# List writes issued per group, the first expert's weight splits behind the routing, and an earlier read of the sums in a fused mixer and expert kernel

## The chip, the cores and the metric

The kernel runs on one core of one Trainium2 chip. The metric is device time in microseconds (us) of one execution; a kernel is run several times, and the median counts. TensorE is called PE, VectorE DVE, ScalarE ACT, GpSimd POOL and SyncE SP, as in the profile.

## The reference

One transformer-like block over 2048 tokens of width 1024. A norm and a projection feed two mixers (a chunked linear-attention mixer and a delta-rule mixer), whose outputs are gated, projected and added to x. Then comes a hierarchical mixture of experts: of 4 groups the best one is taken, in it the best 2 of 8 experts, by softmax weights. Cut to what matters here:

```
x   = x + gt1 * (mixed @ w_out)
h2  = rmsnorm(x, norm2_g) * (1 + sc2) + sh2
lg  = h2 @ wg_r + bg_r;   grp = argmax(lg);   p_grp = softmax(lg)[grp]
pe  = softmax((h2 @ we_r + be_r)[grp]);       top2 of pe -> experts, weights
for each expert e and each token t sent to it:
    hid = silu(h2[t] @ w_gate[e]) * (h2[t] @ w_up[e])     # 1024 -> 512
    out[t] += weight * (hid @ w_down[e])                  # 512 -> 1024
x   = x + gt2 * out
return rmsnorm(x, final_g)
```

All is float32. There are 32 experts, and each has three weight matrices of 2 MB.

## The kernel before

A product in float32 is made of three matmuls on rounded halves: a matrix W is split into `whi` (ACT's cast) and `wlo` (DVE's subtraction W - whi). `Moe.halves` does this for a piece of 128 x 1024; an expert has 12 pieces (`RING` = 12 pairs of halves are kept), four rows of gate and up each and four of down.

The kernel has three phases that matter here. **Mid** (class `Mid`) goes over 16 tiles of 128 tokens: `tile(i)` multiplies by w_out, `after(j)` writes the row block to `X2` (in the profile: X), transposes it, makes the norm and the routing logits `lg`, and writes h2 to `H2` (H). When a group of tiles of `GROUPS` = (0,4), (4,4), (8,4), (12,2), (14,1), (15,1) (first tile, count) has its logits, `route` makes a long chain of small DVE instructions: softmax, best group, best two experts, the mask `M` of chosen experts, with two PE products the place of each token in its expert's list, and from it the row numbers `di`. For each tile two indirect DMAs on POOL then write the token number and weight into the list of its expert in memory (`LIST`), 32 writes in all. The order of instructions in Mid is set by a scheduler.

**Moe.run** follows, whose order is as written. SP loads the first three experts' lists; POOL gathers the first expert's rows of h2 by its list (`gather`) into `gx`; PE transposes them (`x_turn`), ACT and DVE split them (`x_split` into xh, xl); then `block(e)` runs for the 32 experts. `past` inside the block runs a further block on tokens beyond 128 (names `ih`, `il`, "inner"), if the expert has so many. Each expert's result y is added to `X2` by an indirect DMA on POOL (`add`).

Weights come through a ring: `load_next` issues a load of one piece (512 KB) into a `raw` tile, `split` turns it into halves, `pump(n)` does n splits and one load behind each. `todo` lists the 32 x 12 pieces and then the 16 row blocks of `X2`, which are loaded only once `summed` is set. `Moe.first`, called in Mid at tile 15, loads `RAW` = 7 pieces and does all 12 splits of the first expert; `LATE` = 8 more raw tiles exist in Moe.run, whose loads are issued on ACT's queue behind the first `x_split`.

**The tail**: as `X2` may be read once the adds are in, its 16 row blocks are normed in groups of four (`split` of e = NE: ACT squares in `roots`, POOL power, DVE multiplication in `norm`, SP write of the output) beside the last expert's block. Expert 29's add had to be in before the reads; expert 30's y is kept and added behind the reads (`late`); expert 31's y is never added to memory. The tokens of experts 30 and 31 are instead gathered from `X2` by their lists (`sums`), 31's y is added in place, they are normed and written over the output rows by an indirect DMA (`place`), in `last_rows`.

Of the kernel before, what the change touches and what calls it, by code (L numbers as in the profile page):

```python
# [6 lines left out]
FP = mybir.dt.float32  # L7
# [4 lines left out]
OP = mybir.AluOpType  # L12
AX = mybir.AxisListType
# [851 lines left out]
class Mid:  # L865
# [103 lines left out]
    def run(s, ctx):  # L969
        s.moe.lasting()  # L970
        s.k.md = s.t = ctx.enter_context(s.k.tc.tile_pool(name="md", bufs=1, side="right"))
        s.rows()
        s.consts()
        xs, n, due = s.xs, len(s.xs), []
        for i in range(n, 17):
            if i < 15:
                s.tokens(i + 1)
            if i < 16:
                xs[i] = s.tile(i)
            if i == 15:  # L980
                s.moe.first()
            for j in [j for j in sorted(xs) if j < i]:
                i0, c = [(i0, c) for i0, c in GROUPS if i0 <= j < i0 + c][0]
                if j == i0:
                    lg = s.t.tile([128, 4, 36], FP, name="lg", bufs=4)
                s.after(j, xs.pop(j), lg[:, j - i0])
                if j == i0 + c - 1:
                    due.append((i0, c, lg))
                if due and (j >= sum(due[0][:2]) - 1 + (0 if due[0][0] > 8 else 3)):
                    route(s.k, *due.pop(0), s.moe.ps)  # L990
        for d in due:
            route(s.k, *d, s.moe.ps)

# [15 lines left out]
def route(k, i0, c, lg, ps):  # L1009

    nc, md = k.nc, k.md
    T = lambda n, *sh: md.tile([128, 4, *sh], FP, name=n, bufs=4)[:, :c]
# [54 lines left out]
    for j, e in enumerate(E):  # L1067
# [12 lines left out]
        for i in range(c):  # L1080
            one = nc.gpsimd.indirect_dma_start(
                out=k.LIST, out_offset=bass.IndirectOffsetOnAxis(ap=di[:, i:i + 1], axis=0),
                in_=row[:, i], in_offset=None)

            for other in k.scat:
                k.tc.declare_no_dep(one.ins, other.ins, reason="other rows")
            k.scat.append(one)


class Moe:  # L1090
    RING, RAW, LATE = 12, 7, 8

# [29 lines left out]
    def first(s):  # L1122

        for _ in range(min(s.RAW, len(s.todo))):
            s.load_next()
        s.pump(s.RING)

# [21 lines left out]
    def counts(s):  # L1149
        pt = s.ps.tile([128, 512], FP, name="tr", bufs=4)  # L1150
        s.nc.tensor.matmul(pt[:, 0:32], s.k.ones, s.k.Msum, start=True, stop=True)
        s.nc.vector.tensor_copy(s.cnt, pt[0:1, 0:32])

        s.nc.vector.tensor_reduce(s.most, pt[0:1, 30:32], AX.X, OP.max)

# [45 lines left out]
    def last_rows(s):  # L1201


        k, nc, NE = s.k, s.nc, s.k.NE
        xs = [s.raws.pop((NE, j)) for j in range(12, 16)]
        rs = s.roots(xs)
        ls = [s.lists[:, e, 0] for e in (NE - 2, NE - 1)]
        gs = [s.sums(l) for l in ls]
        y = s.own()
        s.norm(xs, rs)  # L1210
        for j, x in enumerate(xs):
            nc.sync.dma_start(s.O[0, (12 + j) * 128:(13 + j) * 128, :], x)
        nc.vector.tensor_tensor(gs[1], gs[1], y, OP.add)
        s.norm(gs)
        for l, x in zip(ls, gs):
            s.place(l, x)

# [48 lines left out]
    def block(s, e, lst, xh, xl, inner=False, mid=None, turn=None):  # L1266
# [14 lines left out]
        for k2 in range(4):  # L1281
            for j, P in enumerate((G, U)):
                prod(P, j, 2 * k2)
                prod(P, j, 2 * k2 + 1)
                if 0 < k2 < 3:
                    pump(1)
            if end and k2 in (1, 2):
                s.pump(4)
            if k2 == 0 and mid:
                mid()  # L1290
                if e == k.NE - 1:
                    s.junk = s.gx[2]
# [22 lines left out]
        if end:  # L1315
            s.pump(4)
            s.late.pop()()
        Y = s.banks(("Y0", "Y1"), inner)
        for kk in range(4):
# [4 lines left out]
            if kk < 3:  # L1324
                pump(1)
        late = e == k.NE - 2 and not inner
        y = s.gx[(e + 1) % 2] if late else s.t.tile([128, 1024], FP, name="y", bufs=2)

# [32 lines left out]
    def run(s, O):  # L1361
# [29 lines left out]
        if NE > 1:  # L1391
            xs.append(first(1))
        hl = s.x_tiles()
        for q in range(2):
            s.x_split(s.x_turn(xs[0], q), *hl, q)
        for _ in range(s.LATE):
            s.load_next(nc.scalar)
        second(0)
        for e in range(NE):
# [43 lines left out]
            hl = nxt  # L1443
            if e >= NE - 3:
                s.summed = True
                while s.loaded < min(s.done + s.RAW + s.LATE, len(s.todo)):
                    s.load_next()
        s.last_rows()

        with tc.If(most > 128):  # L1450
            for e in (NE - 2, NE - 1):
                n = nc.values_load(s.cnt[0:1, e:e + 1], min_val=0, max_val=2048)
# [118 lines left out]
```

## Time and profile before

| | |
|---|---|
| median of three runs | 2954.5 us (2951.3 to 2956.52) |
| the profiled execution | 2948.01 us, of which the span from first to last instruction 2946.2 us |
| mean granted clock of PE in it | 0.967 |
| PE busy | 2724.7 us, 92% of the span |
| DVE / ACT / POOL busy | 2013.0 / 1274.6 / 798.2 us |
| bytes moved | 734.25 MB, mean 249 GB/s |

The profiled execution is one run, somewhat below the median of the three others. Busy shares are means over phases with different limits; what a change is worth is read at its own place. In the profile an instruction's row gives its start and its duration, the tile it writes and reads, and in brackets how long its engine had been idle before it and what released it.

### The profile page before, as it was taken

How to read it: one execution, taken by the hardware profiler on the slowest of the kernel's cores; microseconds unless marked ns; L12 is line 12 of the kernel's file. 1: busy time of each engine (PE TensorE's matmuls, PEld its weight loads, DVE VectorE, ACT ScalarE, POOL GpSimd, SP SyncE). 2: the span in 40 equal slices, each digit the busy share in tenths (PEclk: the TensorE clock that was granted, in tenths of full speed). 3: DMA queues.
4: the chain of work that ended last, by engine and by line, in shares of the span. 5: the costliest groups of instructions: out<-in, count | busy, mean ns of one | idle time of the engine just before them, and what ended most of it. 6: DMA issues, size and time to landing. Idle time of an engine off the chain costs nothing. (4 is left out here: it accounts for less than half of the span.)

```text
span 2946.2 us, 45527 instructions
## 1 busy us (share of the span) xinstructions
PE 2724.7 (92%) x15434; PEld 2245.7 (76%) x15434; DVE 2013.0 (68%) x4136; ACT 1274.6 (43%) x2183; POOL 798.2 (27%) x983
## 2 busy tenths in 40 slices
PE   6989999999999999999999999899958999999993
PEld 5767787878888888888888878688857777777772
DVE  6374775683676656587647886436565699988984
ACT  4333443342333523333333544322225577767763
POOL 2011322322332312342233343322341112111111
PEclk9989999999999999999999989999979999999996
DMA  8999775577565776566665767976448799999996
GB/s 268 305 335 286 236 236 166 181 240 230 158 209 183 235 240 206 179 219 206 203 198 172 233 207 255 345 271 216 144 151 257 272 364 367 362 331 370 366 320 249
DMA packets 460586, 734.25 MB, mean 249 GB/s; under 512 B 115553, under 2 KB 277345, under 8 KB 460242
## 3 DMA queue, kind: packets, MB, share of 16 engines
q1 hardware_dynamic: 448114, 696.68, 70.7%
q0 software_dynamic: 10976, 29.21, 4.3%
q10 hardware_dynamic: 1152, 4.19, 0.4%
q8 instruction: 164, 2.69, 0.4%
q14 instruction: 180, 1.47, 0.2%
HBM read 561.81 MB, written 175.00 MB: 250 GB/s over the span
## 5 line engine op out<-in xcount | busy, mean ns | idle before, releaser
L778 PE MATMUL mm<-hThi,w 128*128 128x512 f32 x1472 | 592.8, 403 | 16.0 <-ACT hThi L667 10.0
L780 PE MATMUL mm<-hThi,w 128*128 128x512 f32 x1472 | 589.5, 401 | 0.2 <-DVE w L761 0.2
L779 PE MATMUL mm<-hTlo,w 128*128 128x512 f32 x1472 | 588.2, 400 | 0.0
L1240 DVE TENSOR_TENSOR wlo<-raw,whi 128x1024 fp32r<-128x1024 f32 x404 | 483.0, 1252 | 45.3 <-ACT whi L1239 29.2
L1239 ACT CAST whi<-raw 128x1024 fp32r<-128x1024 f32 x408 | 405.6, 1057 | 204.0 <-PE U L931 47.9
L778 PEld LDWEIGHTS mm<-hThi,w 128*128 128x128 f32 x1472 | 280.4, 190 | 85.2 <-ACT hThi L667 10.1
L780 PEld LDWEIGHTS mm<-hThi,w 128*128 128x128 f32 x1472 | 280.4, 191 | 65.2 <-DVE w L761 6.6
L779 PEld LDWEIGHTS mm<-hTlo,w 128*128 128x128 f32 x1472 | 280.2, 190 | 57.4 <-DVE hTlo L668 0.7
L1340 POOL DMA_INDIRECT X<-y,lists x32 | 70.8, 2213 | 484.7 <-DVE y L1332 447.5
L243 DVE TENSOR_TENSOR pr<-Pl,Nl 128x2 f32<-128x2 f32 (+30 forms) x496 | 184.9, 373 | 11.7
L451 POOL TENSOR_TENSOR Xq<-h,kf 128x256 f32<-128x256 f32 x96 | 80.1, 834 | 379.7 <-ACT h L448 128.8
L761 DVE TENSOR_TENSOR w<-wraw,w 128x512 fp32r<-128x512 f32 x108 | 80.5, 746 | 106.6 <-ACT w L760 106.6
L760 ACT CAST w<-wraw 128x512 fp32r<-128x512 f32 x108 | 66.6, 619 | 163.4 <-DMA wraw<-in_w_in_dram 103.7
L244 DVE TENSOR_REDUCE Pl<-pr 128x1 f32<-128x2 f32 (+30 forms) x496 | 124.3, 251 | 12.6
L296 PE MATMUL xy<-UV,Gc 128*64 128x64 f32 (+1 forms) x1536 | 115.3, 225 | 3.0 <-ACT UV L305 3.0
L1270 PE MATMUL G<-whi,xh 128*128 128x512 f32 x256 | 104.1, 407 | 11.3 <-PEq L1413 8.6
L296 PEld LDWEIGHTS xy<-UV,Gc 128*64 128x64 f32 (+1 forms) x1536 | 97.2, 128 | 20.2 <-issue 5.9
L856 PE MATMUL mm<-hThi,w 128*128 128x512 f32 x256 | 104.1, 410 | 7.6 <-DMA w<-Ww_proj_b 2.6
L857 PE MATMUL mm<-hTlo,w 128*128 128x512 f32 x256 | 103.9, 406 | 2.6 <-DVE hTlo L668 2.6
L858 PE MATMUL mm<-hThi,w 128*128 128x512 f32 x256 | 102.3, 400 | 0.0
L1270 PE MATMUL G<-whi,xl 128*128 128x512 f32 x256 | 100.7, 393 | 0.0
L1270 PE MATMUL G<-wlo,xh 128*128 128x512 f32 x256 | 100.6, 393 | 0.0
(495 smaller groups left out, 5798.9 us busy)
## 6 DMA issues: line engine op xcount, KB each, us to landing
raw<-in_exp_w_gate_dram SPq DMA_DIRECT2D x126, 512.0 KB
raw<-in_exp_w_up_dram SPq DMA_DIRECT2D x126, 512.0 KB
raw<-in_exp_w_down_dram SPq DMA_DIRECT2D x124, 512.0 KB
w<-Whg SPq DMA_DIRECT2D x96, 512.0 KB
w<-Wgt SPq DMA_DIRECT2D x96, 512.0 KB
w<-Wrw SPq DMA_DIRECT2D x84, 512.0 KB
wraw<-in_w_in_dram SPq DMA_DIRECT2D x92, 256.0 KB
Whg<-w SPq DMA_DIRECT2D x32, 512.0 KB
```

The costliest lines, as they stand in the source:

```text
L243: nc.vector.tensor_tensor(pv, Pl[:, :ni, :ns], Nl[:, :ns, t_][:, None, :].to_broadcast([128, ni, ns]), OP.mult)
L244: nc.vector.tensor_reduce(Pl[:, :ni, t_], pv, AX.X, OP.add)
L296: mm = lambda *a_, **kw: nc.tensor.matmul(*a_, skip_group_check=True, **kw)
L778: nc.tensor.matmul(pt, whi, hi[kk // 2][:, kk % 2], start=(kk == 0), stop=False)
L779: nc.tensor.matmul(pt, whi, lo[kk // 2][:, kk % 2], start=False, stop=False)
L780: nc.tensor.matmul(pt, wlo, hi[kk // 2][:, kk % 2], start=False, stop=(kk == 7))
L856: nc.tensor.matmul(pt, w[:, 0, kk], hi[o // 2][:, o % 2], start=(kk == 0), stop=False)
L857: nc.tensor.matmul(pt, w[:, 0, kk], lo[o // 2][:, o % 2], start=False, stop=False)
L858: nc.tensor.matmul(pt, w[:, 1, kk], hi[o // 2][:, o % 2], start=False, stop=(kk == 3))
L1239: s.nc.scalar.copy(hi, raw)
L1240: eng.tensor_tensor(lo, raw, hi.bitcast(FP), OP.subtract)
L1270: mm = lambda *a, **kw: nc.tensor.matmul(*a, skip_group_check=True, **kw)
```

## The change

It has three parts. First, `route` returns its LIST writes as functions instead of issuing them; `Mid.run` issues them group by group, groups of four are routed two tiles earlier, a group of fewer is routed at once even if another came due at the same tile, and writes that come due at tile 14 are held to tile 15. Second, `Moe.first` only loads; the 12 splits of the first expert stand in Moe.run, six ahead of the first `x_split` and six behind it, and the `LATE` loads (7 now) are issued on SP right behind the list loads. Third, `X2` is read behind expert 28's add; experts 29 and 30 are both kept and added behind the reads (POOL, in the last block), three lists are gathered, two of them are normed in the last block, and the last one behind it.

```diff
@@ class Mid: run
+                while due and (j >= sum(due[0][:2]) - 1 + (0 if due[0][0] > 8 else 1)):
+                    rows += route(s.k, *due.pop(0), s.moe.ps)
+                if j < 14 or j == 15:
+                    for r in rows:
+                        r()
+                    rows = []
-                if due and (j >= sum(due[0][:2]) - 1 + (0 if due[0][0] > 8 else 3)):
-                    route(s.k, *due.pop(0), s.moe.ps)
-        for d in due:
-            route(s.k, *d, s.moe.ps)
@@ route
         for i in range(c):
-            one = nc.gpsimd.indirect_dma_start(
-                out=k.LIST, out_offset=bass.IndirectOffsetOnAxis(ap=di[:, i:i + 1], axis=0),
-                in_=row[:, i], in_offset=None)
...
+            def write(di=di[:, i:i + 1], row=row[:, i]):
+                one = nc.gpsimd.indirect_dma_start(
+                    out=k.LIST, out_offset=bass.IndirectOffsetOnAxis(ap=di, axis=0), in_=row, in_offset=None)
...
+            out.append(write)
+    return out
@@ class Moe
-    RING, RAW, LATE = 12, 7, 8
+    RING, RAW, LATE = 12, 7, 7
@@ first
         for _ in range(min(s.RAW, len(s.todo))):
             s.load_next()
-        s.pump(s.RING)
@@ counts
-        s.nc.vector.tensor_reduce(s.most, pt[0:1, 30:32], AX.X, OP.max)
+        s.nc.vector.tensor_reduce(s.most, pt[0:1, 29:32], AX.X, OP.max)
@@ last_rows
+        x, y = s.parts[2], s.own()
+        for l, p in zip(s.last, s.parts[:2]):
+            s.place(l, p)
+        s.nc.vector.tensor_tensor(x, x, y, OP.add)
+        s.norm([x])
+        s.place(s.last[2], x)
-        xs = [s.raws.pop((NE, j)) for j in range(12, 16)]
-        rs = s.roots(xs)
-        ls = [s.lists[:, e, 0] for e in (NE - 2, NE - 1)]
-        gs = [s.sums(l) for l in ls]
-        y = s.own()
-        s.norm(xs, rs)
-        for j, x in enumerate(xs):
-            nc.sync.dma_start(s.O[0, (12 + j) * 128:(13 + j) * 128, :], x)
-        nc.vector.tensor_tensor(gs[1], gs[1], y, OP.add)
-        s.norm(gs)
-        for l, x in zip(ls, gs):
-            s.place(l, x)
@@ block
-            if end and k2 in (1, 2):
+            if end and k2 == 1:
                 s.pump(4)
+            if end and k2 == 2:
+                s.last = [s.lists[:, i, 0] for i in range(k.NE - 3, k.NE)]
+                s.parts = [s.sums(l) for l in s.last]
             if k2 == 0 and mid:
                 mid()
...
+                if end:
+                    s.pump(4)
+                    for a in s.late:
+                        a()
                 pump(2)
...
         if end:
-            s.pump(4)
-            s.late.pop()()
+            s.pump(8)
+            s.norm(s.parts[:2])
...
-        late = e == k.NE - 2 and not inner
+        late = k.NE - 3 <= e < k.NE - 1 and not inner
@@ run
         for e in range(min(NE, 3)):
             nc.sync.dma_start(lists[:, e], rows[:, e, 0:4])
+        for _ in range(s.LATE):
+            s.load_next()
...
         hl = s.x_tiles()
+
+        s.pump(s.RING // 2)
         for q in range(2):
             s.x_split(s.x_turn(xs[0], q), *hl, q)
-        for _ in range(s.LATE):
-            s.load_next(nc.scalar)
+        s.pump(s.RING - s.RING // 2)
         second(0)
...
-            if e >= NE - 3:
+            if e >= NE - 4:
                 s.summed = True
```

Where instructions stand now is seen in their order on each engine. On POOL at the end of Mid, the order before is (DMA LIST is a list write, xrs the last step of a tile's norm, lrow the rows to write):

```order
L87 TENSOR_TENSOR xrs<-rst_m,mhalf 128x1 x2
L1081 DMA LIST<-lrow_20371,di_20369 67712x4 x4
L1081 DMA LIST<-lrow_20387,di_20385 67712x4 x4
L1079 TENSOR_SCALAR lrow_20513<-wt_20480 128x2
L1079 TENSOR_SCALAR lrow_20527<-wt_20482 128x2
...
L1081 DMA LIST<-lrow_20513,di_20511 67712x4 x2
L1081 DMA LIST<-lrow_20613,di_20611 67712x4
L1081 DMA LIST<-lrow_20527,di_20525 67712x4 x2
L1081 DMA LIST<-lrow_20626,di_20624 67712x4
L1081 DMA LIST<-lrow_20711,di_20709 67712x4
L1081 DMA LIST<-lrow_20724,di_20722 67712x4
```

and in the changed kernel:

```order
L1085 DMA LIST<-lrow_20096,di_20094 67712x4 x4
L1085 DMA LIST<-lrow_20108,di_20106 67712x4 x4
L1082 TENSOR_SCALAR lrow_20301<-wt_20268 128x2
L1082 TENSOR_SCALAR lrow_20313<-wt_20270 128x2
L1059 TENSOR_TENSOR aside<-aside,zero 128x2
L87 TENSOR_TENSOR xrs<-rst_m,mhalf 128x1
L1085 DMA LIST<-lrow_20301,di_20299 67712x4 x2
L1085 DMA LIST<-lrow_20313,di_20311 67712x4 x2
...
L1085 DMA LIST<-lrow_20506,di_20504 67712x4
L1085 DMA LIST<-lrow_20518,di_20516 67712x4
...
L1085 DMA LIST<-lrow_20637,di_20635 67712x4
L1085 DMA LIST<-lrow_20649,di_20647 67712x4
```

The eight writes of group (8,4) moved ahead of the last tile's xrs, and the writes of (12,2), (14,1) and (15,1) each stand behind their own group's rows. On DVE the chains of these three groups were mixed with each other; now they stand one behind the other, (14,1)'s whole chain of 47 rows (37 up to its M) ahead of the logits of tile 15, and 47 more behind those; on PE the transposes of tile 15 stand behind the products with (14,1)'s M.

On DVE between the routing and the first expert's inner block, before:

```order
L1376 MEMSET gx_20743 128x1024
L1152 CAST cnt<-tr 1x32
L1154 TENSOR_REDUCE most<-tr 1x1
L1382 UNCONDITIONAL_BRANCH
L1261 TENSOR_TENSOR xl<-tr,xh 128x512 x2
L1400 TENSOR_LOAD cnt
L1413 COMPARE_AND_BRANCH
L1261 TENSOR_TENSOR il<-tr,ih 128x512 x2
```

and in the changed kernel:

```order
L1381 MEMSET gx_20685 128x1024
L1156 CAST cnt<-tr 1x32
L1158 TENSOR_REDUCE most<-tr 1x1
L1236 TENSOR_TENSOR wlo<-raw,whi 128x1024 x6
L1387 UNCONDITIONAL_BRANCH
L1257 TENSOR_TENSOR xl<-tr,xh 128x512 x2
L1236 TENSOR_TENSOR wlo<-raw,whi 128x1024
...
L1236 TENSOR_TENSOR wlo<-raw_20677,whi 128x1024
L1406 TENSOR_LOAD cnt
L1419 COMPARE_AND_BRANCH
L1257 TENSOR_TENSOR il<-tr,ih 128x512 x2
```

Six splits came to stand between the count of tokens and xl, and six more between xl and il; before, all twelve stood among the last tiles of Mid.

On POOL in the last block and behind it (frs is the power step of a norm), before:

```order
L87 TENSOR_TENSOR frs<-rst_h,mhalf 128x4 x3
L1340 DMA X_79<-gx_20742,lists 2176x1024
L87 TENSOR_TENSOR frs<-rst_h,mhalf 128x4
L1191 DMA raw_41384<-X_79,lists 128x1024
L1191 DMA raw_41388<-X_79,lists 128x1024
L87 TENSOR_TENSOR frs<-rst_h,mhalf 128x2
L1198 DMA out_dram<-raw_41384,lists 2048x1024
L1198 DMA out_dram<-raw_41388,lists 2048x1024
```

and in the changed kernel:

```order
L87 TENSOR_TENSOR frs<-rst_h,mhalf 128x4
L1343 DMA X_79<-ylate,lists 2176x1024
L1343 DMA X_79<-gx_20684,lists 2176x1024
L87 TENSOR_TENSOR frs<-rst_h,mhalf 128x4
L1195 DMA raw<-X_79,lists 128x1024
L1195 DMA raw_41289<-X_79,lists 128x1024
L1195 DMA raw_41293<-X_79,lists 128x1024
L87 TENSOR_TENSOR frs<-rst_h,mhalf 128x4 x2
L87 TENSOR_TENSOR frs<-rst_h,mhalf 128x2
L1202 DMA out_dram<-raw,lists 2048x1024
L1202 DMA out_dram<-raw_41289,lists 2048x1024
L87 TENSOR_TENSOR frs<-rst_h,mhalf 128x1
```

Two adds stand between the first and the second power step, and the three gathers between the second and the third; the third list's write follows as the last row.

## Rows read from the trace of the kernel before

**Rows 1.** Windows: busy us (instructions) by engine, granted clock, DMA share, GB/s.
```profile
2187.00:2205.00 18.00, 3.19 (x12) 2.68 (x12) 5.68 (x49) 0.00 (x0) 13.34 (x22) 0.50 0.02 2
...
2360.00:2840.00 480.00, 447.49 (x2011) 361.49 (x2011) 429.77 (x480) 338.50 (x432) 91.05 (x48) 0.99 1.00 359
```

**Rows 2.** Timeline of POOL at the end of routing: start, duration, instruction, [idle before].
```profile
2182.52 1.07 POOL L1081 DMA_INDIRECT LIST<-lrow,di  x1 [7.09 <-DVE E L1049]
...
2202.91 0.96 POOL L1081 DMA_INDIRECT LIST<-lrow,di  x1 [0.31 <-issue]
...
2207.92 1.06 POOL L1244 DMA_INDIRECT gx<-H,lists  x1 [1.47 <-DMA lists<-LIST]
```

**Rows 3.** Timeline of DVE, end of routing and first expert.
```profile
2189.65 0.34 DVE L1069 TENSOR_REDUCE d<-pt 128x2 f32<-128x64 f32 x2
...
2191.00 0.19 DVE L1049 TENSOR_TENSOR E<-ogq,o2q 128x32 f32<-128x32 f32 x1 [0.92 <-DVE M L1057]
...
2192.47 0.15 DVE L1045 TENSOR_SCALAR zero<-wt 128x1 f32<-128x1 f32 x1 [1.06 <-DVE di L1073]
...
2197.55 0.15 DVE L1073 CAST di<-d 128x1 int32<-128x1 f32 x1 [0.26 <-DVE d L1071]
...
2207.57 0.12 DVE L1152 CAST cnt<-tr 1x32 int32<-1x32 f32 x1
...
2214.48 1.42 DVE L1261 TENSOR_TENSOR xl<-tr,xh 128x512 fp32r<-128x512 f32 x2 [6.73 <-ACT xh L1260]
...
2219.80 1.29 DVE L1261 TENSOR_TENSOR il<-tr,ih 128x512 fp32r<-128x512 f32 x2 [3.90 <-ACT ih L1260]
```

**Rows 4.** Timeline of PE: tile 15's transposes, first expert, first matmul with il.
```profile
2165.06 1.04 PE L947 MATMUL tr<-ident,raw 128*128 128x128 f32 x8
...
2212.61 1.95 PE L1255 MATMUL tr<-ident,gx 128*128 128x128 f32 x8 [16.28 <-DMA gx<-H,lists]
...
2220.55 0.50 PE L1270 MATMUL tr<-whi,il 128*128 128x512 f32 x1
```

**Rows 5.** Timelines of POOL, PE and DVE in the expert loop.
```profile
2845.30 1.47 POOL L1244 DMA_INDIRECT gx<-H,lists  x1 [0.77 <-PE U L1270]
...
2850.19 0.63 PE L1255 MATMUL tr<-ident,gx 128*128 128x128 f32 x4
...
2862.99 6.90 DVE L1240 TENSOR_TENSOR wlo<-raw,whi 128x1024 fp32r<-128x1024 f32 x6 [0.29 <-DVEq L1413]
```

**Rows 6.** Timeline of POOL behind the expert loop.
```profile
2861.85 2.32 POOL L1340 DMA_INDIRECT X<-y,lists  x1 [15.09 <-DVE y L1332]
...
2888.19 1.05 POOL L87 TENSOR_TENSOR frs<-rst_h,mhalf 128x4 f32<-128x4 f32 x1 [24.02 <-DVE rst_h L86]
...
2908.41 2.50 POOL L1340 DMA_INDIRECT X<-gx,lists  x1 [0.31 <-issue]
...
2918.00 2.17 POOL L1191 DMA_INDIRECT raw<-X,lists  x1 [3.73 <-DMA out_dram<-raw]
2920.47 1.02 POOL L1191 DMA_INDIRECT raw<-X,lists  x1 [0.31 <-issue]
...
2932.87 1.82 POOL L1198 DMA_INDIRECT out_dram<-raw,lists  x1 [1.61 <-DVE raw L1176]
2937.74 0.99 POOL L1198 DMA_INDIRECT out_dram<-raw,lists  x1 [3.04 <-DMA out_dram<-raw,lists]
```

**Rows 7.** Timelines of SP, ACT and DVE behind the expert loop.
```profile
2868.73 1.28 SPq L1164 DMA_DIRECT2D raw<-X  x3
...
2883.21 1.06 ACT L1183 ACTIVATE gx<-raw 128x1024 f32<-128x1024 f32 x1 [4.69 <-ACTq L1413]
...
2889.28 4.87 DVE L1176 SCALAR_TENSOR_TENSOR raw<-raw,frs,gx 128x1024 f32<-128x1024 f32 x4 [1.17 <-POOL frs L87]
...
2927.72 1.23 DVE L1213 TENSOR_TENSOR raw<-raw,y 128x1024 f32<-128x1024 f32 x1 [8.54 <-issue]
...
2931.29 2.48 DVE L1176 SCALAR_TENSOR_TENSOR raw<-raw,frs,gx 128x1024 f32<-128x1024 f32 x2 [0.91 <-POOL frs L87]
```

More of the change, by code (lines that the diff above doesn't have):

```diff
@@ L973, in run @@
         s.consts()
-        xs, n, due = s.xs, len(s.xs), []
+        xs, n, due, rows = s.xs, len(s.xs), [], []
         for i in range(n, 17):
@@ L1009, in route @@
 def route(k, i0, c, lg, ps):
-    nc, md = k.nc, k.md
+    nc, md, out = k.nc, k.md, []
     T = lambda n, *sh: md.tile([128, 4, *sh], FP, name=n, bufs=4)[:, :c]
@@ L1080, in route @@
         for i in range(c):
-            one = nc.gpsimd.indirect_dma_start(
-                out=k.LIST, out_offset=bass.IndirectOffsetOnAxis(ap=di[:, i:i + 1], axis=0),
-                in_=row[:, i], in_offset=None)
-            for other in k.scat:
-                k.tc.declare_no_dep(one.ins, other.ins, reason="other rows")
-            k.scat.append(one)
+            def write(di=di[:, i:i + 1], row=row[:, i]):
+                one = nc.gpsimd.indirect_dma_start(
+                    out=k.LIST, out_offset=bass.IndirectOffsetOnAxis(ap=di, axis=0), in_=row, in_offset=None)
+                for other in k.scat:
+                    k.tc.declare_no_dep(one.ins, other.ins, reason="other rows")
+                k.scat.append(one)
+            out.append(write)
+    return out
 class Moe:
-    RING, RAW, LATE = 12, 7, 8
+    RING, RAW, LATE = 12, 7, 7
     def __init__(s, k, I, ctx):
@@ L1201, in last_rows @@
     def last_rows(s):
-        k, nc, NE = s.k, s.nc, s.k.NE
-        xs = [s.raws.pop((NE, j)) for j in range(12, 16)]
-        rs = s.roots(xs)
-        ls = [s.lists[:, e, 0] for e in (NE - 2, NE - 1)]
-        gs = [s.sums(l) for l in ls]
-        y = s.own()
-        s.norm(xs, rs)
-        for j, x in enumerate(xs):
-            nc.sync.dma_start(s.O[0, (12 + j) * 128:(13 + j) * 128, :], x)
-        nc.vector.tensor_tensor(gs[1], gs[1], y, OP.add)
-        s.norm(gs)
-        for l, x in zip(ls, gs):
-            s.place(l, x)
+        x, y = s.parts[2], s.own()
[4 more added lines that the diff above has]
+        s.place(s.last[2], x)
     def again(s, lst):
@@ L1325, in block @@
                 pump(1)
-        late = e == k.NE - 2 and not inner
-        y = s.gx[(e + 1) % 2] if late else s.t.tile([128, 1024], FP, name="y", bufs=2)
+        late = k.NE - 3 <= e < k.NE - 1 and not inner
+        y = s.gx[(e + 1) % 2] if e == k.NE - 2 and not inner else s.t.tile([128, 1024], FP, name="ylate") if late else s.t.tile([128, 1024], FP, name="y", bufs=2)
         def own():
@@ L1450, in run @@
         with tc.If(most > 128):
-            for e in (NE - 2, NE - 1):
+            for e in (NE - 3, NE - 2, NE - 1):
                 n = nc.values_load(s.cnt[0:1, e:e + 1], min_val=0, max_val=2048)
```

## The prediction

> **What bounds the kernel now.** I read the busy times first: PE is busy 92% of the span, so only places where PE idles can give time. The windows show two kinds of stretch [rows 1]. In the expert loop PE is busy 447 of 480 us, DVE 430, and the DMA engines never rest; nothing of the change enters there except through one raw tile less (LATE 8 to 7). At the end of routing, from 2187 to 2205, PE works 3.2 of 18 us, DVE 5.7, and the DMA engines nothing, while POOL is busy 13.3 us.
>
> The timelines then show what is waited for. POOL issues sixteen list writes from 2182.52 to 2202.91, 1.27 us apart at best, each 0.96 us long; the gather of the first expert follows at 2207.92 [rows 2]. DVE has its last di at 2197.55, so there the writes are the bound, by 5 us [rows 3]. PE has finished tile 15 at 2165 and turns the gathered rows at 2212.61 after 16.28 us of idling [rows 4]. From there the path is xl at 2214.48, il at 2219.80, the first matmul with il at 2220.55, and then PE is full. Behind the loop the end is set by the chain add, gathers, norm, two writes of output rows: add at 2908.41, gathers from 2918.00, writes at 2932.87 and 2937.74, and 8.5 us after the last one the span ends [rows 6]. So the change touches two exposed stretches, the transition and the tail, and everything between them is shifted as a block.
>
> **The change: transition.** *List writes.* Eight writes of (8,4) move ahead of the last tile's xrs and run while PE does tiles 14 and 15. What is left behind is the chain of (14,1), then tile 15's logits, then the chain of (15,1), one behind the other. I cost this serial path, since the writes no longer bound it. The writes of (8,4) should start about 2160 (their places need PE products that now stand inside tiles 14 and 15; 2165 is where PE had finished [rows 4]) and take 10.2 us, half of the sixteen's 20.4 [rows 2]; xrs, h2 of tile 15 and the places of (12,2) put the logits of tile 14 at about 2175.5. A step of the chain costs about 0.2 us: from below its own duration, about 0.17; from above 0.25, as 31 steps took 7.9 us from 2189.65 to 2197.55 [rows 3]. (14,1) up to M: 37 steps, 7.4 us, and two trips to ACT, 1.0. Then PE's products, eight transposes (1.95 as at 2212.61 [rows 4]), ACT's copies and the logits: 5.4 us. (15,1): 8.4 up to M, and 2.5 for a PE product and the remaining steps. Sum 24.7, the last di at 2200.2, two writes behind it, the last starting at 2201.8 against 2202.91: **1.1 us earlier**. With 84 steps at 0.17 or 0.25 it is 3.6 earlier or 3.1 later. The large saving on the writes is thus mostly spent on running the chains one after another.
>
> *Seven loads on SP* (0.52 MB each, a piece of 128x1024 floats) now run beside the first gather. In the expert loop a gather issued at 2845.30 is turned by PE 4.9 us later without PE idling [rows 5], at 359 GB/s of other traffic; in the transition it took 4.7. So the price is 0.2 us; bounds 0 and 1.5 (its own 0.52 MB once more at 359 GB/s). x_turn comes at 2211.7.
>
> *Twelve splits* leave the last tiles of Mid, where they lay beside other waits, and stand behind the count. Six cost 6.90 us [rows 5]. The count, 4.66 us behind the last write [rows 2, 3], comes at 2206.5; the first six end at 2213.4, about when xl could start anyway (2211.7 plus the 1.87 between turn and xl before, 2213.6). Their cover is the wait for the gather. The other six start behind xl (1.42) at 2215.0 and end at 2221.9, and only then does DVE reach il, at 2222.0 against 2219.80. ACT's six casts end about the same time. So the **transition costs 2.2 us**. Bounds: lists 3.6 earlier and gather free, il at 2219.4, a gain of 0.4; lists 3.1 late and gather 1.5, il at 2227.3, a loss of 7.5. The ACT queue loses eight load issues, but il was held by the turn on PE there, not by them. One raw tile less costs nothing while ACT, 338 of 480 us busy [rows 1], has slack to take a piece late; without that cover one late piece is 1.5 us.
>
> **The change: tail.** The reads of X2 now wait for expert 28's add. Rows read earlier do not help the first norm unless ACT starts earlier: it began its squares at 2883.21, 4.69 us idle, and the releaser named is the branch, not a row [rows 7]. I leave it there, so the first power step ends at 2889.2 as before [rows 6]. Then POOL issues expert 29's add and must wait for it to land before expert 30's (both change X), and again before the gathers. From an add's start to what needs it: 6.9 us for expert 29 (2861.85 to the read at 2868.73 [rows 6, 7]) and 9.6 for the late one (2908.41 to 2918.00 [rows 6]). Taking 8.25 twice, the gathers start at 2905.8; 2.5 to the second, 1.3 to the third, which ends at 2910.6. The second power step stands behind the second add, which waits for the first: 2897.6 + 2.5 + 1.0, so the second norm runs from 2901 to 2906 and holds hid, queued behind it on DVE, and with hid the last matmuls; these have until DVE comes to y at 2926.6, so this delay is covered. The third power step comes behind the gathers, at 2911.7; two norms of 4.87 with 1.2 to 1.3 between end at 2922.8, two gathered rows take 1.3 + 2.5, to 2926.6. The last rows of the other norm are out at 2926.3 (3.5 us to issue and land, from the 3.04 behind the first write [rows 6]), so the first write starts at 2926.4, the next 4.87 later each [rows 6]: 2931.3, 2936.1. y, its addition (1.23) and norm are done by about 2933, ahead of it. 2936.1 against 2937.74: **the tail gains 1.6 us**. Bounds: adds at 9.6 each, 2.7 later, a loss of 1.1; ACT starting 4.6 earlier and adds at 6.9, last write at 2928.7, a gain of 9.0.
>
> **Sum.** +2.2 - 1.6 = +0.6. The profiled execution of 2948.0 becomes 2948.6. Its own time lies 6.5 us under the median of the runs, 2954.5; on that footing 2955.1, so **2955**. What can be told from no change is about 0.2%, 5.9 us.
>
> **Rivals.**
> *Both ends at their better bounds* (faster): chains at 0.17 a step, the gather free, ACT's squares earlier. -0.4 - 9.0 = -9.4: 2945. For it: ACT had nothing to do at 2878 to 2883, and the named releaser of that idle time is no data. Against: the adds in series on POOL, and 9.6 us for the only add that ran without other traffic.
> *The writes hold DVE* (slower). From 2189 on DVE's dependent steps show gaps of 0.92 and 1.06 us beside POOL's writes of 0.96 [rows 2, 3], as if a step waited for a whole write. Six writes, of (12,2) and (14,1), now run beside the serial chains, where no other chain fills the gaps: 6 x 0.96 = 5.8 us. Lists 4.7 late, il at 2227.8, +8.0 - 1.6 = +6.4: 2961. It decides slower from five and a half writes on. Against it: 49 instructions ran on DVE in those 18 us beside POOL's 13.3 busy us [rows 1], and few of them waited. The Trainium skill (SBUF — State Buffer, "SBUF: two separate sides") states that DVE and GpSimd share a port pair under an exclusive lock, which whoever starts first keeps for the whole instruction, while the other waits. By that rule the sum would be this rival's 2961; this trace bears it out in a few gaps only, so it is a rival here and not the forecast.
> *The first gather queues behind the seven loads* (slower): 10.2 us of loads at 359 GB/s, less the 1.1 between their issue and the gather's: 9.1. x_turn at 2220.6, il at 2230.9, +11.1 - 1.6 = +9.5: 2964. It decides from 5.5 us of lateness. Against it is the loop's gather [rows 5], but there SP's queue is not filled seven deep at once.
>
> **How the numbers follow.** Forecast with its own spread (2951 to 2960): 0.55. Better ends: 0.20, nearly all faster. Writes holding DVE: 0.15, of it two thirds beyond the line. Queued gather: 0.10. That makes faster 0.21, same 0.57, slower 0.22. Leaving out about one in ten on each side gives 2947 to 2962.
>
> **What would show it.** After: the last list write near 2202 relative to an unchanged tile 15; twelve wlo splits of 6.9 us around xl, il some 2 us late; the first gather landing in about 5 us; two adds on POOL behind the first power step 7 to 10 us apart, the third norm behind three gathers, three output writes 4.9 apart. It is wrong if PE's turn comes before 2208 or after 2218, or if the last output write leads or trails the old one by more than 4 us.

## The result, and the profile after

The changed kernel takes 2972.27 us (median of 8 runs, 2964.07 to 2977.17) against 2951.14 us for the kernel before (8 runs on the same chip, 2946.77 to 2956.52): a ratio of 1.0065, with a 95% interval of 1.0052 to 1.0079. By that ratio, which is taken over all runs, it is slower by 0.65%; the medians themselves lie 21.1 us (0.72%) apart. It lies 10 us above the predicted range. Its profiled execution took 2971.76 us with a span of 2969.7 us, 23.5 us more than the span before.

Two executions of the same code are not at the same place when the changed part begins. So I first look for a landmark ahead of the change: the first step of the first group's routing on DVE, in the kernel before

```profile
2019.94 0.17 DVE L1014 TENSOR_REDUCE gm<-lg 128x4 f32<-128x16 f32 x1
```

and in the changed one (start, duration, instruction, and in brackets the idle time before it and its releaser, here as below):

```profile
2024.51 0.17 DVE L1017 TENSOR_REDUCE gm<-lg 128x4 f32<-128x16 f32 x1
```

That is 4.57 us of difference that I do not count as the change's: in the fourteen traces of this document the same row stands anywhere between 2017.04 and 2032.76, and no edit changes what stands ahead of it. All comparisons below are taken from this row on. What is left of the span's 23.5 us is 18.9.

The windows over the same stretches as in [rows 1]:

```profile
2187.00:2205.00 18.00, 7.26 (x32) 6.84 (x32) 9.98 (x74) 1.79 (x5) 2.97 (x8) 0.50 0.09 30
2360.00:2840.00 480.00, 447.30 (x2012) 361.13 (x2011) 428.66 (x479) 338.62 (x432) 90.97 (x48) 0.99 1.00 359
```

The expert loop is the same to 0.2 us of PE. At the end of routing POOL is no longer the busy engine (2.97 us instead of 13.34), DVE is. POOL's timeline there, which answers to [rows 2]:

```profile
2194.24 1.02 POOL L1085 DMA_INDIRECT LIST<-lrow,di  x1 [3.31 <-DVE di L1076]
2195.56 0.96 POOL L1085 DMA_INDIRECT LIST<-lrow,di  x1 [0.30 <-issue]
2206.89 1.00 POOL L1085 DMA_INDIRECT LIST<-lrow,di  x1 [3.31 <-DVE di L1076]
2208.19 0.96 POOL L1085 DMA_INDIRECT LIST<-lrow,di  x1 [0.30 <-issue]
...
2213.22 7.47 POOL L1240 DMA_INDIRECT gx<-H,lists  x1 [1.40 <-DMA lists<-LIST]
2220.99 0.99 POOL L1240 DMA_INDIRECT gx<-H,lists  x1 [0.31 <-issue]
```

The writes now wait for di, not for each other. The last one is 5.28 us later than before, 0.7 beyond the landmark's shift. Then comes what nobody had asked for: the first gather occupies POOL for 7.47 us instead of 1.06. DVE's timeline, answering to [rows 3]:

```profile
2206.30 0.15 DVE L1076 CAST di<-d 128x1 int32<-128x1 f32 x1
...
2212.76 0.12 DVE L1156 CAST cnt<-tr 1x32 int32<-1x32 f32 x1
2212.87 6.88 DVE L1236 TENSOR_TENSOR wlo<-raw,whi 128x1024 fp32r<-128x1024 f32 x6
2230.07 1.43 DVE L1257 TENSOR_TENSOR xl<-tr,xh 128x512 fp32r<-128x512 f32 x2 [10.32 <-ACT xh L1256]
2231.75 6.90 DVE L1236 TENSOR_TENSOR wlo<-raw,whi 128x1024 fp32r<-128x1024 f32 x6 [0.26 <-ACT whi L1235]
2238.57 1.28 DVE L1257 TENSOR_TENSOR il<-tr,ih 128x512 fp32r<-128x512 f32 x2
```

The gather starts 0.35 us behind the first of six splits and is done 0.94 us behind the last. PE's timeline, answering to [rows 4], with the two trips of the masks M of the last two tiles:

```profile
2171.22 0.39 PE L932 MATMUL Y<-whi,wlo 128*128 128x512 f32 x1
...
2191.38 0.60 PE L1065 MATMUL tr<-M,before 128*128 128x32 f32 x2 [8.38 <-DVE M L1060]
...
2204.04 0.61 PE L1065 MATMUL tr<-M,before 128*128 128x32 f32 x2 [6.36 <-DVE M L1060]
...
2228.19 1.96 PE L1251 MATMUL tr<-ident,gx 128*128 128x128 f32 x8 [22.20 <-DMA raw<-in_exp_w_up_dram]
...
2239.30 0.50 PE L1266 MATMUL tr<-whi,il 128*128 128x512 f32 x1 [1.58 <-DVE il L1257]
```

The turn comes 15.0 us behind the gather's start (4.7 in [rows 2, 4]), and the first product with il is 18.75 us later, 14.2 beyond the landmark's shift. The end, answering to [rows 6]:

```profile
2913.64 2.11 POOL L1343 DMA_INDIRECT X<-ylate,lists  x1 [1.91 <-issue]
2922.41 1.57 POOL L1343 DMA_INDIRECT X<-gx,lists  x1 [6.67 <-DMA X<-ylate,lists]
2929.68 1.27 POOL L1195 DMA_INDIRECT raw<-X,lists  x1 [4.62 <-issue]
...
2952.96 1.06 POOL L1202 DMA_INDIRECT out_dram<-raw,lists  x1 [3.13 <-DVE raw L1180]
2957.08 0.98 POOL L1202 DMA_INDIRECT out_dram<-raw,lists  x1 [3.06 <-DVE rst_h L86]
2961.10 1.03 POOL L1202 DMA_INDIRECT out_dram<-raw,lists  x1 [2.44 <-DMA out_dram<-raw,lists]
```

Expert 28's add starts 19.33 us later than before (2861.69 against 2842.36), so the loop added 0.6. From that add to the end of the span it is 108.0 us instead of 103.8: 4.2 more. About 2.5 of these are a single wait in the block behind it (DVE's splits waited 2.77 us there, 0.29 before). A series of waits of 2.2 to 2.8 us, some 120 us apart, stands in both traces, with five in each (before the change at 2343.24, 2462.48, 2581.49, 2703.50 and 2823.32; behind it at 2384.72, 2504.65, 2624.19, 2745.08 and 2865.32). Only the last one has moved across expert 28's add. Counted alike, the loop lost 3.1 us and the tail 1.7. The sum is 14.2 + 3.1 + 1.7 = 19.0, which is the 18.9, as it must be, since the three pieces cover the span.

Of the loop's 3.1, 1.7 lie in the first expert, whose add comes 21.3 us behind the first product with il instead of 19.6. PE had waited 1.61 us for ih and 1.58 for il, and just behind il its products become slow, which they do not before:

```profile
2221.12 0.40 PE L1270 MATMUL tr<-wlo,ih 128*128 128x512 f32 x1
```

```profile
2239.97 0.63 PE L1266 MATMUL tr<-wlo,ih 128*128 128x512 f32 x1
```

Over the ten us behind the first il PE's granted clock is 0.83 in the changed kernel and 1.00 before: for a part of them PE was back at the lower of its two levels (1.2 instead of 2.4 GHz).

### The profile page after: what moved, and what is told of

Its sections match the earlier page's. It is cut to its first block, busy times and chain, and to the rows that moved or that the text cites. A ratio compares the mean times of both kernels' runs of the same rounds, so it can differ in the third digit from the quotient of the medians.

```text
span 2969.7 us, 45553 instructions
## 1 busy us (share of the span) xinstructions
PE 2734.9 (92%) x15434; PEld 2250.2 (76%) x15434; DVE 2016.2 (68%) x4138; ACT 1277.6 (43%) x2185; POOL 808.6 (27%) x986
## 5 line engine op out<-in xcount | busy, mean ns | idle before, releaser
L778 PEld LDWEIGHTS mm<-hThi,w 128*128 128x128 f32 x1472 | 282.3, 192 | 85.9 <-ACT hThi L667 10.3
L761 DVE TENSOR_TENSOR w<-wraw,w 128x512 fp32r<-128x512 f32 x108 | 79.7, 738 | 105.8 <-ACT w L760 103.8
```

The costliest lines, as they stand in the source:

```text
L778: nc.tensor.matmul(pt, whi, hi[kk // 2][:, kk % 2], start=(kk == 0), stop=False)
```

## Experiments

Every time is set against runs of the kernel before on the same chip. The ratio in the table is taken over all runs, as in the result, with its 95% interval in the text; it is not exactly the quotient of two medians. To read the front of every run alike I take four distances from its trace: from the first row of routing (above) to PE's last product with w_out; from that to the gather's start; from there to PE's turn; from the turn to the first product with il. In us:

```
                    Mid    to gather  to turn  to il    all    ratio
before             144.9     43.1       4.7     7.9    200.6   1
changed            146.7     42.0      15.0    11.1    214.8   1.0065
lists_only         146.8     50.8       4.9     9.3    211.8   1.0038
splits_only        144.9     38.5      14.7    11.1    209.1   1.0022
tail_only          144.9     43.4       4.9     7.6    200.8   1.0006
twelve_behind      146.7     40.1       9.1    17.9    213.8   1.0074
loads_late         146.7     41.3      11.4    21.1    220.5   (one run)
gaps               146.7     40.1       9.2    15.3    211.3   (one run)
paced              146.7     40.1       8.8    11.1    206.7   (one run)
one_between        146.7     41.4      15.0    11.1    214.2   (one run)
routes_last        146.8     37.8       4.9     9.0    198.4   1.0002
after_routes       146.7     28.6      14.4    11.1    200.8   1.0001
mended             146.8     30.5       4.9    12.1    194.2   0.9999
front_only         146.8     32.9       5.0    12.2    196.8   1.0002
```

**Each part alone.** *lists_only*: the kernel before with the changed `Mid.run` and `route`, the splits still in `first`.

> The kernel before with the list writes and the earlier routing alone; the twelve splits stay in Mid, the loads on ACT, the tail as before. Theory (the loss arises at the first gather, beside the splits and loads that now run there): POOL's first gather takes 1.0 to 1.1 us as before, the total is within 3 us of the kernel before (2948 to 2954). Rival (the routing, run as one chain after another, is what costs): the last list write comes 5 us or more later relative to tile 15's last product and the total is 5 to 10 us above before.

Measured: 2962.7 us, ratio 1.0038 [1.0023, 1.0053], slower by 10: the rival's forecast, not the theory's. The gather is as quick as before; the routing is 7.7 us longer and Mid 1.9. PE's timeline shows the two masks one behind the other:

```profile
2193.44 0.61 PE L1064 MATMUL tr<-M,before 128*128 128x32 f32 x2 [6.36 <-DVE M L1059]
...
2206.11 0.61 PE L1064 MATMUL tr<-M,before 128*128 128x32 f32 x2 [6.36 <-DVE M L1059]
```

12.7 us apart; the kernel before had its last two such products, each behind a wait for M, at 2191.21 and 2194.34.

*splits_only*: the kernel before with the splits behind the routing and the seven loads on SP.

> The kernel before with the twelve splits behind the routing and the seven loads behind the list loads, nothing else. Theory: POOL's first gather is stretched to 6 to 8 us, PE turns its rows 14 to 16 us after its issue (4.7 before), and the total is 12 to 16 us above before. Rival (routing costs): the gather is stretched only together with the rest, and the total is within 5 us of before.

Measured: 2959.96 us, ratio 1.0022 [1.0009, 1.0035], 7.6 us above before, so the 12 to 16 of the theory were a miss, while the gather came as it said. With DVE free of splits the routing of before ends 4.6 us earlier, but POOL's row of the gather is the stretched one:

```profile
2202.56 7.48 POOL L1243 DMA_INDIRECT gx<-H,lists  x1 [1.30 <-DMA lists<-LIST]
```

*tail_only*: the kernel before with the changed tail and LATE = 7.

> The kernel before with the tail part alone (sums read behind expert 28's add, two adds behind the reads, three gathers in the last block, LATE 7). Theory: the tail gives nothing back: counted from the last product with gate and up, the last output row is written at the same time as before within 2 us, the block before the last loses about 2 us to the reads of the sums, total 0 to 4 us above before. Rival (the tail was mis-sized in my forecast by its adds): total 5 us or more above before, with more than 9.6 us between the adds.

Measured: 2953.01 us, ratio 1.0006 [0.9996, 1.0017]: no change that can be told. In the trace the time from the last product of gate and up (2887.30) to the last output row (2938.58) is 51.3 us, before 49.7 (2888.00 to [rows 6]): 1.5 longer. ACT's timeline says why:

```profile
2908.57 0.80 ACT L1310 CAST hh<-tr 128x256 fp32r<-128x256 f32 x2 [15.42 <-PE tr L1307]
```

Before, it stood 7.2 us earlier:

```profile
2901.35 0.80 ACT L1310 CAST hh<-tr 128x256 fp32r<-128x256 f32 x2 [8.18 <-PE tr L1307]
```

hh waits for hid, hid stands on DVE behind the second norm, that behind the second power step, and that on POOL behind the second add. The third norm's squares stand on ACT behind hh and start only at 2909.26.

**What stretches the gather.** *twelve_behind*: the changed kernel with all twelve splits behind xl, the loads still ahead.

```diff
-        s.pump(s.RING // 2)
         for q in range(2):
             s.x_split(s.x_turn(xs[0], q), *hl, q)
-        s.pump(s.RING - s.RING // 2)
+        s.pump(s.RING)
```

> The changed kernel with all twelve splits behind the first x_split; the seven loads stay on SP behind the list loads, beside the gather. If the splits hold POOL (DVE's run of six without a gap): the first gather takes about 1 us again and PE turns its rows 5 to 9 us after its issue. If the loads hold it: the gather still takes 6 us or more. In both cases il waits for twelve splits, 13.8 us, so that the total stays within 5 us of the changed kernel's 2972.

Measured: 2974.69 us, ratio 1.0074 [1.0061, 1.0087]. The rows of POOL and PE:

```profile
2208.30 1.06 POOL L1240 DMA_INDIRECT gx<-H,lists  x1 [1.43 <-DMA lists<-LIST]
...
2217.39 1.95 PE L1251 MATMUL tr<-ident,gx 128*128 128x128 f32 x8 [16.34 <-DMA gx<-H,lists]
```

With no splits beside it the gather is issued in 1.06 us although SP's loads are running; but PE turns its rows 9.1 us behind its start, 4.4 more than before. The six splits more behind xl use up what is won.

*loads_late*: the six splits beside the gather without their loads; all loads behind `x_split` on ACT's queue.

> The changed kernel with no weight load ahead of the first x_split: six splits stay beside the gather, the thirteen loads go out on ACT behind the split of x. If the splits hold POOL, the first gather still takes 7 us or more, and PE turns its rows 10 to 12 us after its issue (less than the changed kernel's 15, since no loads share the DMA engines). If loads and splits are both needed for it, the gather takes about 1 us.

Measured, one run: 2976.84 us. The gather took this on POOL, and the turn came 11.4 us behind its start:

```profile
2205.95 7.50 POOL L1240 DMA_INDIRECT gx<-H,lists  x1 [1.36 <-DMA lists<-LIST]
```

So the splits alone hold POOL, and the loads add some 4 us to the landing.

*gaps*: in the changed kernel, each of the first six splits waits for a copy by ACT that reads the split before.

```diff
+            if last is not None:
+                nc.scalar.copy(hi[:, 0:512], last[:, 0:512].bitcast(FP))
             nc.scalar.copy(hi, raw)
             nc.vector.tensor_tensor(lo, raw, hi.bitcast(FP), OP.subtract)
+            last = lo
```

> The changed kernel with the first six splits in a round trip: ACT overwrites half of the next whi with the split before it and then makes the right cast, so that DVE waits for ACT between two splits (about 1.6 us of gap). Theory (DVE's run of six splits without a pause keeps POOL out until its end): POOL's first gather gets in behind one split and takes 1 to 2.5 us. Rival (any split in flight delays the gather's own work, in proportion): the gather takes 4 us or more. The first six splits end about 9 us later than in the changed kernel; the total is no test here.

Measured, one run: 2971.49 us. DVE's and POOL's rows:

```profile
2210.84 1.20 DVE L1409 TENSOR_TENSOR wlo<-raw,whi 128x1024 fp32r<-128x1024 f32 x1
2213.80 1.23 DVE L1409 TENSOR_TENSOR wlo<-raw,whi 128x1024 fp32r<-128x1024 f32 x1 [1.76 <-ACT whi L1408]
```

```profile
2211.20 1.78 POOL L1240 DMA_INDIRECT gx<-H,lists  x1 [1.41 <-DMA lists<-LIST]
```

The same six splits, with 1.76 us between them, hold the gather for the rest of one split: it ends 0.94 us behind the first split, as it ended 0.94 us behind the sixth in the changed kernel. In this pair it is the run without a pause that is long. But this edit adds two things, a pause and a cast to wait for, and in the expert loop gathers inside runs of six without a pause take 1.0 to 2.1 us. Two more runs take these apart.

*paced*: the first six casts on ACT are held until the count is there, so that each split follows its cast, with nothing between two splits.

```diff
+        nc.vector.tensor_copy(ct, s.cnt)
...
+            nc.scalar.copy(hi[0:1, 0:32], ct)
             nc.scalar.copy(hi, raw)
```

> The changed kernel, with the casts of the first six pieces on ACT held back until the count is there (each reads 32 floats that are made of the count), so that DVE's six splits follow ACT's casts as they do in the expert loop, where gathers of 1.0 to 2.1 us stand inside such runs of six; nothing else lies between two splits. What is open: the splits of the changed kernel had their casts long before, those of the run called gaps had both a pause and a cast to wait for. Theory A (a split that has to wait for its cast lets POOL in, however short the wait): the gather takes 1 to 2.5 us, although the splits fill 7 to 8 us. Theory B (any run of splits that starts together with the gather holds it until a pause of a microsecond): 6.5 to 7.5 us.

Measured, one run: 2967.65 us. Rows of POOL, then of DVE:

```profile
2214.14 1.05 POOL L1240 DMA_INDIRECT gx<-H,lists  x1 [1.40 <-DMA lists<-LIST]
2215.51 0.99 POOL L1240 DMA_INDIRECT gx<-H,lists  x1 [0.31 <-issue]
2216.80 0.99 POOL L1240 DMA_INDIRECT gx<-H,lists  x1 [0.30 <-DVE wlo L1409]
```

```profile
2215.56 7.20 DVE L1409 TENSOR_TENSOR wlo<-raw,whi 128x1024 fp32r<-128x1024 f32 x6 [1.56 <-ACT whi L1408]
```

The first gather was through before the first split, so it tells nothing of A; the two others stand beside the run, which takes 7.20 us instead of 6.88, some 0.05 a split for its cast, and neither was held. PE's first il came 8 us earlier than in the changed kernel by the table.

*one_between*: a memset of 128x1 on DVE behind each of the first six splits, their casts long done.

> The changed kernel with a memset of 128x1 on DVE behind each of the first six splits, whose casts are done long before, as in the changed kernel: no wait for another engine, but another instruction, of some 0.1 us and with no second operand, between two splits. Theory (POOL gets its turn at any instruction of DVE that does not use both operands from SBUF): the gather takes 1 to 2.5 us. Rival (only an idle DVE lets POOL in): 7 to 8 us, until the last of the six is done.

Measured, one run: 2965.08 us.

```profile
2205.10 7.56 POOL L1240 DMA_INDIRECT gx<-H,lists  x1 [1.35 <-DMA lists<-LIST]
```

The rival's forecast came: another instruction between two splits (0.06 us each) does not let POOL in. Its reason, that only an idle DVE does, is not shown by this, and the gathers of the expert loop speak against it.

**How the groups are routed.** *routes_last*: lists_only, but the last three groups are routed together behind tile 15; (8,4)'s writes stay early.

```diff
-                while due and (j >= sum(due[0][:2]) - 1 + (0 if due[0][0] > 8 else 1)):
+                while due and (j == 15 or due[0][0] < 9 and j > sum(due[0][:2]) - 1):
```

> The kernel with the list writes per group alone, but the last three groups are routed together behind tile 15, so that their chains can mix on DVE again. Theory (one chain after another is what cost lists_only its 10 us): the last list write starts 6 to 11 us earlier than in lists_only relative to tile 15's last product, the first expert no later than before, and the total is within 4 us of the kernel before (2948 to 2954), possibly some us below, since the eight writes of group (8,4) no longer stand in front of the last eight. Rival (the cost of lists_only comes from the eight writes beside the last tiles, not from the order of the chains): the total stays 7 us or more above before.

Measured: 2951.07 us, ratio 1.0002 [0.9991, 1.0013]: the 10 us of lists_only are gone. *after_routes* makes the same edit in the changed kernel and undoes nothing else.

> The changed kernel, with one thing undone: the last three groups of tiles are routed together behind tile 15, as before the change; splits, seven loads and tail stay as changed. Theory (the three causes add up: chains in series about +10 us, splits and loads at the first gather about +7.6, tail about +0.7): 21.1 less 10 leaves +11, a median near 2962; the gather still takes 7.4 to 7.5 us to issue and PE's turn comes 14 to 15.5 us behind its start. Rival A (the parts are not independent: the shorter routing only moves the gather to where it has to wait for DVE and the loads all the same): less than 5 us come back, 2967 or more. Rival B (routing is what counts, the gather's wait was hidden by something else): 2953 or less.

Measured: 2949.03 us, ratio 1.0001 [0.9987, 1.0015]. My theory's 2962 was a miss; the whole loss is gone, with the gather as slow as ever. PE's and POOL's rows:

```profile
2186.21 0.64 PE L1065 MATMUL tr<-M,before 128*128 128x32 f32 x2 [6.86 <-DVE M L1060]
...
2187.12 0.60 PE L1065 MATMUL tr<-M,before 128*128 128x32 f32 x2
...
2212.35 1.95 PE L1251 MATMUL tr<-ident,gx 128*128 128x128 f32 x8 [23.22 <-DMA raw<-in_exp_w_up_dram]
```

```profile
2192.97 0.96 POOL L1085 DMA_INDIRECT LIST<-lrow,di  x1 [0.30 <-issue]
...
2198.00 7.47 POOL L1240 DMA_INDIRECT gx<-H,lists  x1 [1.31 <-DMA lists<-LIST]
```

The error was to take lists_only's +10 as the price of the serial order. It is a net figure. The table has all four cases: from the last w_out product to the gather, serial against together is 50.8 against 37.8 with the splits in Mid, and 42.0 against 28.6 without them: 13.0 and 13.4. The theory's "gather" part held to the digit, rival B's reason (a hidden gather) did not: the wait is paid, from 14.5 us that the earlier writes and the free DVE give.

*mended* takes both causes away: routing together, eight splits in Mid and four behind xl, loads on ACT as before. *front_only* is that without the changed tail.

```diff
+        s.pump(8)
...
-        s.pump(s.RING // 2)
...
+        for _ in range(s.LATE):
+            s.load_next(nc.scalar)
+        s.pump(4)
-        s.pump(s.RING - s.RING // 2)
```

> The changed kernel with both causes taken away: the last three groups routed together, eight of the first expert's splits back among Mid's last tiles, none ahead of the first x_split, the other four behind it, and the seven loads again on ACT's queue behind x_split. Early list writes and the changed tail stay. Theory: POOL issues the gather in about 1.06 us and PE turns 4.7 to 5.2 us behind it; four splits behind xl (4.6 us of DVE) make il about 0.7 us later against xl than before; Mid ends about 1.8 us earlier for the four splits that left it; with the tail's +0.7 to +2.3 the median is within 3 us of before (0.999 to 1.001). Rival (something else of the change costs time, the tail's extra stall in the loop above all): 3 to 6 us slower than before, with transition rows as in the kernel before. Rival (the room of routing and splits adds up to a gain): 3 to 6 us faster than before.

> The kernel before with its front alone changed, as the runs so far recommend it: list writes per group, the last three groups routed together behind tile 15, eight of the twelve splits left in Mid and four behind the first x_split, loads and tail as before. Theory: the first matmul with il comes some 6 us earlier, measured from tile 3 of Mid on (in the run with the changed tail besides it was 6.4), and the old tail is 1 to 2 us shorter than the changed one, so the median is 4 to 6 us below before (0.998 to 0.9986). Rival (the loop gives the 6 us back, because it waits for weights that do not come earlier, whatever the front does): within 2 us of before, with longer idle times of PE between the experts than in before. Rival (the tail was what cost the 6 us in that run): 7 us or more below before.

Measured: mended 2948.9 us, ratio 0.9999 [0.9986, 1.0012]; front_only 2951.73 us, ratio 1.0002 [0.9986, 1.0018], its 12 runs spread from 2934.54 to 2962.53. In mended the gather is quick again:

```profile
2200.89 1.06 POOL L1241 DMA_INDIRECT gx<-H,lists  x1 [1.61 <-DMA lists<-LIST]
...
2205.79 1.95 PE L1252 MATMUL tr<-ident,gx 128*128 128x128 f32 x8 [14.88 <-DMA gx<-H,lists]
```

The traces show the first il 6.4 and 3.8 us earlier than before, by the table, but the medians do not show it: front_only's theory of 4 to 6 us was a miss. From the first il product to the end of the span mended takes 733.4 us, front_only 731.1, before 725.7 and after_routes 723.2: what the front gave, these two executions lost later. A part of it has a row. As in the changed kernel, PE had waited (3.7 us in mended, 4.5 in front_only, for ih and il), and its granted clock over the ten us behind the first il was 0.83 and 0.71, with products of 0.63 us. The first expert's add comes 21.2 and 22.2 us behind il, 19.6 before: 1.6 and 2.6 us of the loss. Whether the rest is chance or also follows an earlier front stays open; front_only's profiled execution was the slowest of its twelve, and stood 12.8 us behind the kernel before at the landmark already. No version here beats the kernel before.

Against after_routes, mended's quick gather brings the first il 6.6 us forward and changes nothing in the ratio (0.9999 against 1.0001). That the gather counts in the changed kernel's time is seen beside the serial chains alone: 1.0038 for lists_only, where it is quick, and 1.0065 for the changed kernel, whose tail by itself gave 1.0006.

## Why the prediction was wrong

**The step that failed** is the price of the first gather: "So the price is 0.2 us; bounds 0 and 1.5". It measured 10.3 (15.0 from issue to turn against 4.7), with two causes. The splits, which I had placed under "the wait for the gather" as their cover, made that wait: 6.4 us on POOL (7.47 against 1.06). The other 3.9 are put down to the seven loads, which cost 4.4 where no split was in the way (twelve_behind, 9.1 against 4.7) and gave back 3.6 when they were taken away (loads_late, 11.4 against 15.0). The expert loop's gather [rows 5], from which I took the 0.2, does stand inside six splits without a pause, from 2845.30 to 2846.77:

```profile
2843.50 6.90 DVE L1240 TENSOR_TENSOR wlo<-raw,whi 128x1024 fp32r<-128x1024 f32 x6 [0.29 <-DVEq L1413]
```

There it was done 0.9 us behind the end of the one split that ran when it began, here 0.94 us behind the last of six. So the row was no measure for the first gather; why it was not is open (last section). il was forecast at 2222.0; less the landmark's 4.57 it came at 2234.0, 12.0 later, and 10.1 of the 12.0 is this term.

**The list writes** were forecast 1.1 us earlier and came 0.7 later: off by 1.8. The logits of tile 14 came 3.0 us later than forecast (2183.05 less the 4.57, against 2175.5); 1.8 of these are the time by which Mid itself grew up to its last w_out product, in every run with this edit. The serial path from there to the last di, forecast at 24.7 us, took 23.3 (2183.05 to 2206.30), and the last write started 0.3 later behind it than forecast. So the size was nearly right, and yet I read it wrongly: I set the serial chains against the eight writes alone, found that they cancel, and did not see that the free DVE gives the routing another 9 us (after_routes against routes_last). By the ratios, undoing the serial order gives the whole loss back (after_routes). In the traces it gives 14.0 us at the front (214.8 against 200.8), as much as the change had lost there. Another 7.2 lie behind the first il (730.4 against 723.2): 1.7 of them are the first expert at the lower clock, the rest no run explains.

**The other six splits** behind xl were forecast to bring il 2.2 us later than before against a turn 0.9 earlier, so 3.1 behind the turn; measured 3.2 (10.4 from turn to il, 7.2 before). Right.

**The tail** was to gain 1.6 us; alone it lost 1.5 in the trace, in the whole 1.7 (2909.65 to 2961.10), and 0.0006 [-0.0004, 0.0017] of the median. The adds are 9.1 and 6.9 us from start to successor in tail_only (8.25 forecast for each) and ACT's first squares stayed where they were, as I said. The failed step is "so this delay is covered": hid's delay holds hh on ACT and with it the squares of the third norm, which I had let start behind the gathers.

**The sum.** The forecast's +0.6 and the traces' 18.9 differ by the 12.0 us of il, by 3.3 of the tail (+1.7 instead of -1.6), and by the 3.1 of the loop, for which the forecast had nothing. Its 2955 also stood on a median of three runs, 2954.5; eight runs gave 2951.14.

**The rivals.** "The first gather queues behind the seven loads" gave 2964 and the right symptom, a turn at 2220.6 (2223.6 less the shift), but the loads are the smaller half of it. "The writes hold DVE" named the right pair of engines and had it the wrong way round: DVE's splits held POOL. The Trainium skill (SBUF — State Buffer, "SBUF: two separate sides") has, beside the lock that I weighed, a box on this very direction, that a DMA issued by GpSimd cannot write its descriptors while DVE runs an operation in a 2-port mode. The lock too is stated there only for such operations and, against a GpSimd operation that reads SBUF, for those with two inputs in SBUF, a condition that the prediction left out. I had not taken the splits as such a case, and which of the two they are no run shows. The gaps run agrees with the box for one split (the gather was done 0.94 us behind it); that a gather waits for a run of six is more than the page states, and the measurement decides.

## What to carry to other kernels

Before work is moved into a wait, look at what the wait is for: a run of DVE instructions with all its data ready, beside a POOL DMA that is still to be issued, is no filler here, and its price can be the length of the whole run. A long chain of small dependent steps should be issued together with its siblings, so that each fills the other's gaps; routing three groups one behind the other, each as soon as it could start, cost 13 us against routing them together, from the last w_out product to the gather. And a part measured alone gives a net figure: only the four cases of two edits showed that the parts were not to be added.

## What the runs showed of the hardware

POOL's indirect DMA took 7.47 to 7.56 us in the five runs that issue it just behind the first of six splits whose casts were long done, and 1.05 to 1.06 in those with none beside it, whether or not 0.5 MB loads were running. A memset between the splits changed nothing; with 1.76 us of idle DVE behind each split it took 1.78, and beside splits that each waited some 0.05 us for a cast (7.20 us for six instead of 6.88), later gathers took 0.99. What stays open: the fourth gather of the changed kernel began 3.9 us into the second run of six, which shows no pause either, and took 1.59 us, done 0.9 us behind the end of the split that ran when it began:

```profile
2235.65 1.59 POOL L1240 DMA_INDIRECT gx<-H,lists  x1 [12.38 <-PE tr L1251]
```

That run's casts were made while it went on, as in the expert loop, where the gathers are as short. Whether the waiting for casts is what lets POOL in there was not shown.

Behind the first product with il, PE's granted clock over ten us was 1.00 in seven of the fourteen traces, and the first expert's add came 19.6 us behind il in each of these. In the other seven (the changed kernel, twelve_behind, loads_late, gaps, one_between, mended and front_only) it was 0.71 to 0.85, and the add came 20.9 to 22.2 us behind il. In these PE had waited 2.6 to 13.2 us for ih and il, in the first seven 0.2 to 2.8. Where the clock fell, a late il cost 1.3 to 2.6 us more than the wait itself.
